# Coupling the rows of each pair once, before the substitution, in the 32x32 inverses of a delta-rule kernel

## The chip, the cores and the metric

The kernel runs on one core of a Trainium2 chip. The metric is the device time of one execution in microseconds, the median of several runs. The engines are named as in the profile: PE is TensorE (matmuls), PEld its weight loads, DVE is VectorE, ACT is ScalarE, POOL is GpSimd, SP is the engine that issues most of the transfers. Each engine works through its own list of instructions in order; the engines wait for each other by semaphores.

## The reference, cut to what matters

One layer of a decoder: 2048 prompt tokens with 1024 channels and 8 sample tokens go through one wide input projection, then through two branches, an RWKV-7 recurrence over 16 heads of 64 channels and a causal convolution with 31 taps, which are gated, added and projected. The change lies in the recurrence:

```python
def wkv7_scan(s0, r, w, k, v, a, b):
    """S_t = S_{t-1} diag(w_t) + (S_{t-1} a_t) b_t^T + v_t k_t^T ;  y_t = S_t r_t"""
    def step(s, inp):
        rt, wt, kt, vt, at, bt = inp
        sa = jnp.einsum('bhij,bhj->bhi', s, at)
        s = s * wt[:, :, None, :] + sa[..., None] * bt[:, :, None, :] + vt[..., None] * kt[:, :, None, :]
        yt = jnp.einsum('bhij,bhj->bhi', s, rt)
        return s, yt
```

The kernel takes the tokens in chunks of 64. Inside a chunk each token's `sa` depends on those of the tokens before it through a strictly lower triangular 64x64 matrix L of products of the a and b rows, so that the inverse of (I - L) is needed for every chunk and head. It is built from the inverses of its two 32x32 diagonal blocks and one product for the block below them. Row t of such an inverse is e_t plus the sum over s < t of L[t, s] times row s: a forward substitution over 32 rows.

## The kernel before

**Tiling.** The prompt is cut into 4 blocks of 512 tokens (`b`), a block into 8 units (`j`) of two heads, 128 channels; so there are 32 units, each with 8 chunks and 2 heads. For a unit, `unit_in` projects r, k, v and the gate (matmuls `pg<-ht,w`, each of three passes over a split into a rounded part and its remainder, 8 tiles deep) and shifts them by a token on ScalarE and VectorE (`raw`). `unit_a` makes decays and keys, the triangular matrices `W` (tile `sc`), the inverses (tiles `gd`, `gp`, `zr`, `zbuf`) and what depends on them only by chunk; `unit_b` runs the state from chunk to chunk (`xs<-pc`) and ends the branch. Between units, `fill` gives other work to the engines: `glu`, `conv_norm`, `conv_gate`, `gate`, and the taps of the convolution, which `pull` deals out on VectorE (`et`). After the 8 units of a block come `merge` and `stage_out`, nearly pure matmul stages. The 8 sample tokens are worked on by `decode` on VectorE in blocks 1 and 2.

**Order.** The program is written unit by unit, but each engine's list is laid down by a planner when the program is built: it takes the instruction with the best priority among those that it thinks ready, on estimates of its own of how long each takes. The priority is the place in the program; `later(n)` puts instructions n places back, `tc.high_priority(n)` n places ahead. The shifts, the GLU and the gates' first steps stand 550 places ahead (`HPS`, `HPU`, `HPG`, `HPZ`), `conv_norm` 200 places back (`LN`), `decode` 500 back (`LD`). So instructions of other helpers stand in VectorE's list between the steps of a substitution, and projection matmuls stand in TensorE's list while it lasts.

**The inverses, L581 to L611.** ScalarE copies the 32x32 diagonal blocks out of `W` into `gd` (L586). One transpose on VectorE (L589) lays them out as `gp[p, t, s]`: the 128 partitions are 4 quadrants (2 heads, 2 diagonal blocks) of 8 chunks with 4 partitions each, and all 4 partitions of a system hold its whole 32x32 matrix. The result `zr[p, i, t]` has 8 of the 32 columns in each of these partitions, column 4 i + d in partition d. L590 sets the diagonal of `gp` to 1, so that the unit vectors in `zr` (L594) come along in each sum. `sub` keeps the 16 entries that couple the second row of a pair to its first, `gp[2 m + 1, 2 m]` (L598), and L599 clears them in `gp`. Then the loop of L600 takes two rows at a time. For rows t and t + 1 one product (L603, tile `gd`, since `pr` lies in it) multiplies all earlier rows with the two rows of `gp`, one reduce (L605) sums over s, and one scalar_tensor_tensor (L606; in the profile L107, `zr<-zr,sub`) adds `sub` times row t to row t + 1. Only `n` of the 8 column groups and `w` of the 32 rows are touched, so that a step grows from 8 to 512 elements. Every step needs the one before it: 15 products, 15 reduces and 16 scalar_tensor_tensor in a row. Two more transposes, L609 and L611, put the result back, and the matmuls `pb<-gd,sc` (L619) are the first that need it.

**Around it.** `zr` has one buffer: GpSimd clears it for the next unit (L593) when L609 has read it, and ScalarE then writes the unit vectors (L594). `pr` and `gd` are one tile with one buffer, and `gp` is one tile with one buffer too.

Of the kernel before, what the change touches and what calls it, by code (L numbers as in the profile page):

```python
# [11 lines left out]
ALU = mybir.AluOpType  # L12
AX = mybir.AxisListType
# [13 lines left out]
def rwkv7_conformer_step(  # L27
# [6 lines left out]
    nc = tc.nc  # L34
# [55 lines left out]
    def new(shape, tag, dt=F32):  # L90
        return sb.tile(shape, dt, name=tag, tag=tag, bufs=BUFS.get(tag, 1))
# [8 lines left out]
    def tt(out, a, b, op):  # L100
        return nc.vector.tensor_tensor(out=out, in0=a, in1=b, op=op)  # L101

    def mul(out, a, b):
        return tt(out, a, b, ALU.mult)

    def stt(out, a, s, b, op0, op1):
        return nc.vector.scalar_tensor_tensor(out=out, in0=a, scalar=s, in1=b, op0=op0, op1=op1)  # L107

    def vcp(out, in_):
        return nc.vector.tensor_copy(out=out, in_=in_)  # L110
# [91 lines left out]
    for e in range(2):  # L202
        s = slice(e * 64, e * 64 + 64)
# [13 lines left out]
    with later(LI):  # L217
# [3 lines left out]
                                axis=AX.X, op=ALU.add)  # L221
        par_p = const.tile([128, 2], F32, name="par_p")
        nc.vector.tensor_reduce(out=par_p, in_=ident.rearrange("p (c d) -> p d c", d=2),
                                axis=AX.X, op=ALU.add)
        par_c = const.tile([128, 2], F32, name="par_c")
        nc.vector.tensor_reduce(out=par_c, in_=ident.rearrange("p (d c) -> p d c", d=2),
                                axis=AX.X, op=ALU.add)
# [275 lines left out]
    def unit_a(b, j, tw, ins):  # L503
# [63 lines left out]
        for hf in range(2):  # L567
            pse = [pa(), pa()]
            for i in range(4):
                c = hf * 4 + i  # L570
# [10 lines left out]
        pr = new([128, 8, 2, 32], "gd")  # L581
# [5 lines left out]
        gp = new([128, 32, 32], "gp")  # L587
        gpf = gp.rearrange("p a b -> p (a b)")
        nc.vector.transpose(out=gp, in_=gd.rearrange("p c j -> p j c").unsqueeze(3).to_broadcast([128, 32, NC, 4]))  # L589
        nc.vector.memset(gpf[:, 0:1024:33], 1.0)  # L590

        zf = new([128, 288], "zr")
        nc.gpsimd.memset(zf, 0.0)  # L593
        cp(zf.rearrange("p (i r) -> p i r", r=36)[:, :, 0:4], grp.unsqueeze(1).to_broadcast([128, 8, 4]))  # L594
        zr = zf[:, 0:256].rearrange("p (i t) -> p i t", t=32)

        sub = new([128, 16], "sub")
        vcp(sub, gpf[:, 32:1024:66])  # L598
        nc.vector.memset(gpf[:, 32:1024:66], 0.0)  # L599
        for t in range(0, 32, 2):  # L600
            n, w = t // 4 + 1, t + 2
            if t:
                mul(pr[:, 0:n, :, 0:w], zr[:, 0:n, 0:w].unsqueeze(2).to_broadcast([128, n, 2, w]),  # L603
                    gp[:, t:t + 2, 0:w].unsqueeze(1).to_broadcast([128, n, 2, w]))
                nc.vector.tensor_reduce(out=zr[:, 0:n, t:t + 2], in_=pr[:, 0:n, :, 0:w], axis=AX.X, op=ALU.add)  # L605
            stt(zr[:, 0:n, t + 1:t + 2], zr[:, 0:n, t:t + 1], sub[:, t // 2:t // 2 + 1], zr[:, 0:n, t + 1:t + 2],  # L606
                ALU.mult, ALU.add)
        zt = gd
        nc.vector.transpose(out=zt.rearrange("p c (i d) -> p i c d", d=4), in_=zr)  # L609
        zv = zbuf[u % 2]  # L610
# [32 lines left out]
        for hf in range(2):  # L643
            ps = pa()
            for i in range(4):
                nc.tensor.transpose(out=ps[:, i * 128:i * 128 + 128],
                                    in_=bk[:, hf * 4 + i, 0:2].rearrange("p a t -> p (a t)"), identity=ident)
# [518 lines left out]
    for b in range(NB):  # L1166
        last = b == NB - 1
        orr = []
        if b == SB - 1:
            work = sample_work()  # L1170
            act(gate_s, gate_s, AF.Exp, scale=-1.0)
            act(gate_s, gate_s, AF.Ln, bias=1.0)
            act(gate_s, gate_s, AF.Exp, scale=-1.0)
        parts = unit_a(b, 0, tw, ins)
        ins = unit_in(b, 1, ht)
        for j in range(HP):
            if j == RJ and not last:
                stage_rms(b + 1)
            orr.append(unit_b(b, j, parts))
            pull(FT)  # L1180
            if j < HP - 1:
                parts = unit_a(b, j + 1, tw, ins)
            if j < HP - 2:
                ins = unit_in(b, j + 2, ht)
            for what in (FILL0 if b == 0 else FILL2 if last else FILL1)[j]:
                fill(b, ht, cs, what)
                pull(FT)
            if b in DW:
                for _ in range(DW[b][j]):
                    with later(LD):  # L1190
                        next(work, None)
# [81 lines left out]
```

## Time and profile before

| | |
|---|---|
| median of 3 runs | 2832.91 us (2832.56 to 2835.99) |
| the profiled execution | 2830.14 us |
| its span, first to last instruction | 2828.4 us |
| mean granted clock of TensorE | 0.987 |
| moved to and from memory | 466.91 MB, 165 GB/s |

The profile is that of one execution. Its busy times are sums over the span and hide which stage is limited by what; its waits tell which engine stood still, and what ended that. A matmul's row is longer than the distance from one to the next, since matmuls overlap. A line such as L107 or L113 is that of a helper which all callers share, so that a group is known by the tiles beside it: `zr<-zr,sub` writes `zr` and reads `zr` and `sub`. In the views, `x480` is a count, and behind the second bar stands the engine's idle time in front of the group's instructions.

### The profile page before, as it was taken

What the parts mean: (1) busy time and instruction counts of PE and PEld (TensorE: products, weight loads), DVE (VectorE), ACT (ScalarE), POOL (GpSimd) and SP (SyncE); (2) the same over time, 40 slices, a digit from 0 to 9 for tenths busy, and PEclk for the clock granted to TensorE, in tenths of its full rate; (3) what the DMA queues carried; (4) which work ended last, traced back from release to release, by engine and by line L of the source; (5) the groups of instructions that cost most, each with busy time, mean ns of one, the idle gap of its engine ahead of it and who ended that gap; (6) DMA issues with size and microseconds to landing.
All of it is one profiled execution on the core that took longest, in us unless ns stands there. A gap on an engine that the chain in (4) does not pass through costs nothing.

```text
span 2828.4 us, 55917 instructions
## 1 busy us (share of the span) xinstructions
PE 2680.2 (95%) x22800; PEld 2129.1 (75%) x22800; DVE 1965.0 (69%) x4560; ACT 1318.7 (47%) x2783; POOL 16.1 (1%) x61
## 2 busy tenths in 40 slices
PE   6999898999999989999999998999999997999988
PEld 6888887878877767777887766777797765777777
DVE  5789898677877667667568667676665767765522
ACT  5555556662344464555113556555312455545511
POOL 0000000000000000000000000000000000000000
PEclk9999999999999999999999999999999998999999
DMA  5555754547964334254665335344475422332474
GB/s 197 202 172 189 209 179 137 182 160 249 316 240 136 105 122 136 100 168 160 215 239 202 106 103 151 116 138 162 160 237 205 156 88 71 108 117 98 135 275 161
DMA packets 153107, 466.91 MB, mean 165 GB/s; under 512 B 19281, under 2 KB 24642, under 8 KB 152843
## 3 DMA queue, kind: packets, MB, share of 16 engines
q1 hardware_dynamic: 145745, 437.55, 46.3%
q10 hardware_dynamic: 7106, 25.79, 2.5%
q8 instruction: 179, 2.93, 0.4%
q14 instruction: 77, 0.63, 0.1%
HBM read 350.41 MB, written 113.35 MB: 164 GB/s over the span
## 4 chain that ended last, share of the span: by engine, by line
PE 53%; DVE 29%; ACT 13%; issue 3%; DMA 2%; SPq 0%; POOL 0%; DVEq 0%; ACTq 0%; POOLq 0%
PE pg L113 34%; PE pa L113 7%; DVE gd L101 5%; DVE zr L605 5%; PE pc L113 4%; PE py L113 4%; DVE zr L107 3%; DVE et L107 3%; ACT sc L95 2%; PE pb L113 2%; DVE raw L107 2%; ACT zbuf L95 2%; ACT xv L95 1%; DVE w L101 1%; ACT tmp L95 1%
## 5 line engine op out<-in xcount | busy, mean ns | idle before, releaser
L113 PE MATMUL pg<-ht,w 128*128 128x512 f32 (+1 forms) x7200 | 1518.6, 362 | 15.1 <-DVE sraw L110 5.3
L113 PEld LDWEIGHTS pg<-ht,w 128*128 128x128 f32 x7200 | 1163.2, 189 | 255.5 <-issue 59.8
L107 DVE SCALAR_TENSOR_TENSOR et<-u,cw,et 128x512 f32<-128x512 f32 x480 | 359.4, 749 | 6.7
L95 ACT ACTIVATE raw<-pg,omm 128x512 f32<-128x512 f32 (+1 forms) x155 | 92.9, 602 | 208.9 <-PE pg L113 201.4
L95 ACT ACTIVATE tmp<-tmp 128x512 f32<-128x512 f32 (+1 forms) x305 | 185.0, 625 | 9.0 <-DVE tmp L526 3.2
L101 DVE TENSOR_TENSOR gd<-zr,gp 128x8 f32<-128x8 f32 (+14 forms) x480 | 179.7, 374 | 11.7
L113 PE MATMUL pg<-orr,w 128*128 128x512 f32 (+2 forms) x960 | 185.0, 349 | 0.0
L605 DVE TENSOR_REDUCE zr<-gd 128x2 f32<-128x8 f32 (+14 forms) x480 | 176.6, 368 | 11.7
L113 PEld LDWEIGHTS pg<-orr,w 128*128 128x128 f32 x960 | 155.2, 188 | 25.1
L95 ACT ACTIVATE w<-wraw 128x512 fp32r<-128x512 f32 x162 | 101.3, 627 | 117.8 <-PE pg L113 75.4
L698 DVE TENSOR_SCALAR xs<-pc,dk 128x64 f32<-128x64 f32 x224 | 63.5, 284 | 111.6 <-PE pc L113 109.3
L95 ACT ACTIVATE sc<-pa 64x256 f32<-64x256 f32 (+1 forms) x192 | 72.9, 380 | 136.4 <-PE pb L113 133.1
L101 DVE TENSOR_TENSOR w<-wraw,w 128x512 fp32r<-128x512 f32 x162 | 111.0, 687 | 32.2 <-ACT w L95 31.5
L107 DVE SCALAR_TENSOR_TENSOR raw<-pg,prm,raw 128x511 f32<-128x511 f32 (+1 forms) x185 | 104.3, 574 | 29.9 <-ACT raw L95 29.3
L107 DVE SCALAR_TENSOR_TENSOR zr<-zr,sub 128x5 f32<-128x5 f32 (+7 forms) x512 | 115.7, 226 | 13.3
L95 ACT ACTIVATE gd<-sc 32x128 f32<-32x128 f32 x256 | 78.4, 306 | 92.2 <-DVE sc L101 89.6
L101 DVE TENSOR_TENSOR x<-x,pg 128x512 f32<-128x512 f32 (+1 forms) x80 | 46.2, 578 | 94.6 <-PE pg L113 56.5
L113 PE MATMUL pa<-ar,bk 64*64 64x128 f32 x2048 | 105.7, 285 | 5.6 <-DVE sc L101 3.2
L113 PEld LDWEIGHTS pa<-ar,bk 64*64 64x64 f32 x2048 | 81.3, 136 | 39.2 <-DVE bk L101 15.2
L101 DVE TENSOR_TENSOR sc<-pa,maskw 128x512 f32<-128x512 f32 x128 | 82.7, 685 | 30.8 <-PE pa L113 30.7
L101 DVE TENSOR_TENSOR keep<-pa,raw 128x512 f32<-128x512 f32 x32 | 22.1, 692 | 113.9 <-PE pa L113 113.9
L113 PE MATMUL pg<-xv,w 128*128 128x512 f32 (+2 forms) x320 | 89.8, 354 | 8.8 <-DVE x L101 8.8
(360 smaller groups left out, 3654.3 us busy)
## 6 DMA issues: line engine op xcount, KB each, us to landing
w<-kept_in SPq DMA_DIRECT2D x366, 512.0 KB, 3.3
kept_in<-w SPq DMA_DIRECT2D x122, 512.0 KB, 4.0
wraw<-in_w_in_dram SPq DMA_DIRECT2D x122, 256.0 KB, 3.2
w<-kept_br SPq DMA_DIRECT2D x48, 512.0 KB, 4.1
w<-kept_out SPq DMA_DIRECT2D x40, 512.0 KB, 4.3
gate<-x ACTq DMA_DIRECT2D x32, 512.0 KB, 4.9
x<-gate SPq DMA_DIRECT2D x64, 256.0 KB, 3.9
w<-kept_bc SPq DMA_DIRECT2D x24, 512.0 KB, 3.5
```

The lines of the kernel that those rows point to most:

```text
L95: return nc.scalar.activation(out=out, in_=in_, func=func, scale=scale, bias=bias, **kw)
L101: return nc.vector.tensor_tensor(out=out, in0=a, in1=b, op=op)
L107: return nc.vector.scalar_tensor_tensor(out=out, in0=a, scalar=s, in1=b, op0=op0, op1=op1)
L113: return nc.tensor.matmul(out=out, lhsT=lhsT, rhs=rhs, start=start, stop=stop, **kw)
L605: nc.vector.tensor_reduce(out=zr[:, 0:n, t:t + 2], in_=pr[:, 0:n, :, 0:w], axis=AX.X, op=ALU.add)
L698: nc.vector.tensor_scalar(out=state[:, j, :] if c == NC - 1 else xs[:, c + 1, :], in0=pu[:, c * C:c * C + C], scalar1=dk[:, c:c + 1], scal ...
```

## The change

The coupling inside each pair is put into the rows of `gp` once, ahead of the loop. For all 16 pairs together, one product makes coupling times first row (into `pr`, 128x16x32), and one addition adds it to the second row. This is done before the diagonal is set to 1, so that the coupling entry itself stays in `gp` and brings in the unit vector of row t; it is no longer cleared. With that, a step's product and reduce give both rows of the pair at once, and the scalar_tensor_tensor is left at t = 0 alone, where there is no product. The copy `sub` and the memset that cleared the entries go.

```diff
         nc.vector.transpose(out=gp, in_=gd.rearrange("p c j -> p j c").unsqueeze(3).to_broadcast([128, 32, NC, 4]))
+
+        both = pr.rearrange("p a b c -> p (a b) c")
+        rows2 = gp.rearrange("p (r i) s -> p r i s", i=2)
+        mul(both, rows2[:, :, 0, :], gpf[:, 32:1024:66].unsqueeze(2).to_broadcast([128, 16, 32]))
+        tt(rows2[:, :, 1, :], rows2[:, :, 1, :], both, ALU.add)
         nc.vector.memset(gpf[:, 0:1024:33], 1.0)
...
-        sub = new([128, 16], "sub")
-        vcp(sub, gpf[:, 32:1024:66])
-        nc.vector.memset(gpf[:, 32:1024:66], 0.0)
-        for t in range(0, 32, 2):
+        stt(zr[:, 0:1, 1:2], zr[:, 0:1, 0:1], gpf[:, 32:33], zr[:, 0:1, 1:2], ALU.mult, ALU.add)
+        for t in range(2, 32, 2):
             n, w = t // 4 + 1, t + 2
-            if t:
-                mul(pr[:, 0:n, :, 0:w], zr[:, 0:n, 0:w].unsqueeze(2).to_broadcast([128, n, 2, w]),
-                    gp[:, t:t + 2, 0:w].unsqueeze(1).to_broadcast([128, n, 2, w]))
-                nc.vector.tensor_reduce(out=zr[:, 0:n, t:t + 2], in_=pr[:, 0:n, :, 0:w], axis=AX.X, op=ALU.add)
-            stt(zr[:, 0:n, t + 1:t + 2], zr[:, 0:n, t:t + 1], sub[:, t // 2:t // 2 + 1], zr[:, 0:n, t + 1:t + 2],
-                ALU.mult, ALU.add)
+            mul(pr[:, 0:n, :, 0:w], zr[:, 0:n, 0:w].unsqueeze(2).to_broadcast([128, n, 2, w]),
+                gp[:, t:t + 2, 0:w].unsqueeze(1).to_broadcast([128, n, 2, w]))
+            nc.vector.tensor_reduce(out=zr[:, 0:n, t:t + 2], in_=pr[:, 0:n, :, 0:w], axis=AX.X, op=ALU.add)
```

## The prediction

> **What bounds the kernel now.** I read the page first: the busy times, then the chain that ended last.
>
> ```profile
> span 2828.4 us, 55917 instructions
> ...
> PE 2680.2 (95%) x22800; PEld 2129.1 (75%) x22800; DVE 1965.0 (69%) x4560; ACT 1318.7 (47%) x2783; POOL 16.1 (1%) x61
> ...
> PE 53%; DVE 29%; ACT 13%; issue 3%; DMA 2%; SPq 0%; POOL 0%; DVEq 0%; ACTq 0%; POOLq 0%
> PE pg L113 34%; PE pa L113 7%; DVE gd L101 5%; DVE zr L605 5%; PE pc L113 4%; PE py L113 4%; DVE zr L107 3%; DVE et L107 3%; ACT sc L95 2%; PE pb L113 2%; DVE raw L107 2%; ACT zbuf L95 2%; ACT xv L95 1%; DVE w L101 1%; ACT tmp L95 1%
> ```
>
> The two views seem to disagree. By busy time TensorE is the bound: it is idle for 2828.4 − 2680.2 = 148 us in all. By the chain, the substitution (gd L101, zr L605, zr L107) holds 5 + 5 + 3 = 13% of the span, some 370 us, on VectorE. Both can be true: a chain follows whoever came last, even by a fraction of a microsecond, and says nothing of how little earlier TensorE could have gone on. So the waits of TensorE decide, and next to them the stretches in which TensorE has work at hand.
>
> ```profile
> PEld pb L113 <- DVE gd L609: 31.2, 27, 4.6
> PE pb L113 <- DVE gd L609: 20.2, 22, 4.1
> ...
> PE pg L113 <- DVE tmp L101: 26.1, 6, 7.0
> ...
> ACT zr L95 <- POOL zr L593: 50.8, 7, 13.1
> ```
>
> (Columns: total us, number of waits, longest.) The end of the substitution is the transpose L609. TensorE waited for it 20.2 us in 22 of the 32 units, 4.1 us at most; its weight loads, which run ahead of the matmuls, 31.2 us. That is what TensorE loses to the substitution in the whole program, out of a chain share of some 370 us. The timeline of TensorE during the substitution shows why; here are the last unit, one with much other VectorE work in between, and an early one:
>
> ```profile
> 2639.63 15.34 PE L113 MATMUL pg<-ht,w 128*128 128x512 f32 x65
> 2656.29 0.69 PE L113 MATMUL pb<-gd,sc 32*32 32x32 f32 x32 [1.32 <-DVE gd L609]
> ...
> 1723.70 2.08 PE L113 MATMUL pg<-tmp,avg_c 128*128 128x512 f32 x2 [6.61 <-DVE tmp L101]
> 1724.79 20.10 PE L113 MATMUL pg<-ht,w 128*128 128x512 f32 x80
> 1745.06 0.69 PE L113 MATMUL pb<-gd,sc 32*32 32x32 f32 x32 [0.16 <-DVE gd L609]
> ...
> 160.57 23.67 PE L113 MATMUL pg<-ht,w 128*128 128x264 f32 x192 [0.17 <-DVE u L107]
> 184.41 0.60 PE L113 MATMUL pg<-ht,w 128*128 128x264 f32 x3 [0.17 <-DVE sraw L110]
> 184.93 0.69 PE L113 MATMUL pb<-gd,sc 32*32 32x32 f32 x32
> ```
>
> Ahead of the first matmul that needs the inverse stands a run of projection matmuls: 65 here, 80 there, 192 narrower ones in the third. TensorE comes to the waiting matmul 1.32 us early, 0.16 us early, or not early at all. The fill is fitted to the length of each substitution: the planner that lays down each engine's order puts in as many matmuls as it thinks the VectorE work lasts. A wait of 1 us is what its estimate misses.
>
> **What the change removes and adds.** For each of 32 units it takes away 15 of the 16 scalar_tensor_tensor (the one at t = 0 stays), the copy of sub and one memset, and adds a product and an addition of 512 elements each: 17 instructions out, 2 in. The durations:
>
> ```profile
> L107 DVE SCALAR_TENSOR_TENSOR zr<-zr,sub 128x5 f32<-128x5 f32 (+7 forms) x512 | 115.7, 226 | 13.3
> ...
> L110 DVE COPY sub<-gp x32: 136/138/141, 90.9 to 2639.2; 128x16 f32<-128x16 f32 x32
> ...
> L599 DVE MEMSET gp<- x32: 72/72/72, 91.1 to 2639.4; 128x16 f32 x32
> ...
> 2637.86 1.25 DVE L589 STREAM_TRANSPOSE gp<-gd 128x1024 f32<-128x1024 f32 x1 [0.73 <-ACT gd L95]
> 2639.18 0.14 DVE L110 COPY sub<-gp 128x16 f32<-128x16 f32 x1
> 2639.20 0.09 DVE L590 MEMSET gp<- 128x32 f32 x1
> 2639.38 0.20 DVE L107 SCALAR_TENSOR_TENSOR zr<-zr,sub 128x1 f32<-128x1 f32 x1
> 2639.40 0.07 DVE L599 MEMSET gp<- 128x16 f32 x1
> 2639.61 0.17 DVE L101 TENSOR_TENSOR gd<-zr,gp 128x8 f32<-128x8 f32 x1
> 2639.81 0.16 DVE L605 TENSOR_REDUCE zr<-gd 128x2 f32<-128x8 f32 x1
> 2640.01 0.22 DVE L107 SCALAR_TENSOR_TENSOR zr<-zr,sub 128x1 f32<-128x1 f32 x1
> 2640.26 0.18 DVE L101 TENSOR_TENSOR gd<-zr,gp 128x24 f32<-128x24 f32 x1
> ...
> 2654.07 0.69 DVE L101 TENSOR_TENSOR gd<-zr,gp 128x512 f32<-128x512 f32 x1
> 2654.80 0.69 DVE L605 TENSOR_REDUCE zr<-gd 128x16 f32<-128x512 f32 x1
> 2655.52 0.23 DVE L107 SCALAR_TENSOR_TENSOR zr<-zr,sub 128x8 f32<-128x8 f32 x1
> 2655.79 0.45 DVE L609 STREAM_TRANSPOSE gd<-zr 128x256 f32<-128x256 f32 x1
> ```
>
> Busy time: 480 × 0.226 = 108.5 us go, with 32 × (0.138 + 0.072) = 6.7 us; the two new operations have no row of their own, the nearest is the 128x512 product above at 0.69 us (same operation, broadcast operands, SBUF), so 64 × 0.69 = 44.2 us come. VectorE falls by 71 us to about 1894 us.
>
> Length of one substitution, in the last unit, where nothing else runs on VectorE: from the end of L589 (2637.86 + 1.25 = 2639.11) to the end of L609 (2655.79 + 0.45 = 2656.24) it is 17.13 us. A scalar_tensor_tensor that goes frees the time to the next start: 2640.26 − 2640.01 = 0.25 in the first such step, 2655.79 − 2655.52 = 0.27 in the last; 15 × 0.26 = 3.9 us. At the head the first one now starts at 2639.38; with the new pair ahead, each holding the next by 0.73 as the product does at 2654.07 (the reduce starts at 2654.80), it starts at 2639.18 + 2 × 0.73 = 2640.64, so 1.26 later. Saved: 3.9 − 1.26 = 2.6 us, a chain of 14.5 us. A bound for the pair, whose rows are picked out with a stride that no row shows:
>
> ```profile
> L107 DVE SCALAR_TENSOR_TENSOR et<-u,cw,et 128x512 f32<-128x512 f32 x480 | 359.4, 749 | 6.7
> ```
>
> At the 0.749 us of this dearer two-step operation of the same size the saving is 0.1 us smaller; the cheapest the pair can be is nothing, and then 1.4 us more are saved. I keep 2.6. The diagonal memset, now behind the pair, costs 0.02 to 0.2 us (2639.18 to 2639.20, or to the next start at 2639.38), inside that bound. No DMA, no ScalarE and no matmul instruction is added or moved. The new product writes the tile that ScalarE filled for L589, which the same engine has read by then, so no wait across engines is added. ScalarE's wait for zr (50.8 us, through GpSimd's memset) hangs on L609 of the unit before and ends sooner with it; it is at no place that TensorE shows as a wait of its own.
>
> **What of it reaches the end.** 32 × 2.6 = 84 us would be saved if TensorE stood still meanwhile. It does not:
>
> ```profile
> core 0: us, PE busy (x) PEld busy (x) DVE busy (x) ACT busy (x) POOL busy (x), PEclk, DMA share, GB/s
> ...
> 640.00:820.00 180.00, 180.00 (x786) 146.96 (x785) 138.37 (x215) 59.65 (x113) 0.00 (x0) 1.00 0.84 292
> ...
> 2639.10:2656.25 17.15, 15.87 (x71) 12.51 (x69) 15.40 (x51) 3.39 (x5) 0.00 (x0) 1.00 0.55 184
> ```
>
> In the 17.15 us of the last substitution TensorE is busy for 15.87, and its 65 matmuls take 15.34 / 65 = 0.236 us each, against 180.0 / 786 = 0.229 us in a stage that does nothing but such matmuls. There is no slack inside that run; only its end, the 1.28 us, can be won. The Trainium skill, "Perfetto Trace Analysis", section Identifying the Most-Contended Engine, holds that matmul busy time is a bad measure of how far TensorE is from its limit and that the share of weight loads should be read. By that share (75% on the page) TensorE would have a quarter of its time free, and the whole 84 us could be had. The rows above speak against it here: the pure matmul stage has weight loads busy for only 146.96 of 180.00 us, 82%, with TensorE never idle.
>
> So the gain is bounded by the waits on L609. If every engine kept its order, each wait would shrink by up to 2.6 us: all 20.2 us except 4.1 − 2.6 = 1.5 of the longest, so 18.7 us (29 us if the weight loads' 31.2 tells the truth). If the order is planned anew, the fill shrinks with the chain, and what remains is how far the plan misses. Were the miss in proportion to the number of the chain's instructions (in a unit 15 products and 15 reduces, the groups below over 32, and 16 scalar_tensor_tensor), removing 15 of 46 would take 33% of 20.2 us, 6.7 us.
>
> ```profile
> L101 DVE TENSOR_TENSOR gd<-zr,gp 128x8 f32<-128x8 f32 (+14 forms) x480 | 179.7, 374 | 11.7
> ...
> L605 DVE TENSOR_REDUCE zr<-gd 128x2 f32<-128x8 f32 (+14 forms) x480 | 176.6, 368 | 11.7
> ```
>  The last unit, with nothing between, misses by 1.32 us, the unit of 20.10 us of fill by 0.16: it is the short steps, not the length, that are underrated, it seems, which puts the value above 6.7. I take the middle of 6.7 and 18.7, 13 us. The matmuls that leave the fill cost nothing; they stand later, where others stand now.
>
> The profiled execution took 2830.14 us, its span and 1.7 us around it; with 13 us less, 2817. It lies 2.8 us below the median of the runs, 2832.91, so for the median 2820.
>
> **The rivals.** (1) The order does not move: 18.7 us, 2814. For it: the priorities are the same and only 15 instructions of a unit go. Against: the fills above follow each chain's length.
> (2) The plan swallows it: the estimates follow the chain, the wait stays about 20 us, the median stays at 2833, within 5.7 us. For it: the wait is much the same in chains of very different fill. This is also how it goes if the new pair, at the head, is dearer than I think.
> (3) The whole chain comes through: 84 us, 2749. For it only the chain of waits; against it the 15.87 busy us.
> (4) Slower: the wait on the convolution's sums. conv_norm's additions share VectorE with one substitution in each block:
>
> ```profile
> 1045.67 0.68 DVE L101 TENSOR_TENSOR tmp<-tmp 128x512 f32<-128x512 f32 x1
> 1046.27 0.22 DVE L107 SCALAR_TENSOR_TENSOR zr<-zr,sub 128x3 f32<-128x3 f32 x1
> ```
>
> TensorE waits for these sums 26.1 us in 6 places, 6.61 us in the row at 1723.70, where its mean-matmul stands ahead of 80 projection matmuls that could run. The new pair is two long operations at the head of just that stretch, and the priorities reach 550 places in a program that is now 15 places shorter per unit, so the plan there can turn. If these waits double, 26 us are lost against 13 won: 2846. It decides once they grow by more than 13; from 19 on the kernel is measurably slower.
>
> **How the numbers follow.** A measurement of this kernel tells 0.2%, 5.7 us. Chances: the forecast 0.38 (its own range 2814 to 2826, from 18.7 to 6.7 us), the fixed order 0.18, the swallowed gain 0.27, the whole chain 0.04, slower 0.13. Faster by over 0.2%: 0.38 + 0.18 + 0.04 = 0.60; the same 0.27; slower 0.13. The range takes in the fixed order with the weight loads' 29 us (2804) and the swallowed gain with its 5.7 us (2839); it leaves out the chain and nearly all of the slower case.
>
> **What would show it.** Two new rows x32 at about 0.69 us, the scalar_tensor_tensor down to x32, a substitution with nothing between of 14.5 us, VectorE at about 1894 us: these test the cost. TensorE's busy time unchanged at 2680 and the wait on the transpose at 7 us instead of 20.2 test the forecast; a wait near 1.5 with the same 65 matmuls ahead of it would be rival 1, a wait near 20 with some 11 matmuls fewer (2.6 / 0.236) rival 2, a longer row of waits for tmp rival 4. The forecast is wrong if the time moves while the wait on the transpose does not.

## The result and the profile after

The kernel after takes 2804.84 us in the median of 4 runs (2802.72 to 2806.61), beside 2834.45 us for the kernel before on the same chip (2832.56 to 2838.42): a ratio of 0.989, with an interval of 0.9878 to 0.9902. That is 29.6 us less, where 13 were forecast; the time lies just inside the low end of the range, 2804 to 2839. The two profiled executions, 2830.14 and 2806.61 us, are 23.5 us apart, since the first is shorter than each of the four timed runs of its kernel and the second is the longest of its own. What follows from the traces accounts for those 23.5 us; the other 6 are in no trace here.

The page of the kernel after, span, busy times and chain:

```profile
span 2804.9 us, 55406 instructions
...
PE 2681.7 (96%) x22800; PEld 2131.4 (76%) x22800; DVE 1906.5 (68%) x4080; ACT 1321.7 (47%) x2783; POOL 16.4 (1%) x61
...
PE 61%; DVE 22%; ACT 12%; DMA 2%; issue 2%; SPq 0%; POOL 0%; DVEq 0%; ACTq 0%; POOLq 0%
PE pg L113 43%; PE pa L113 7%; DVE gd L101 5%; PE pc L113 4%; PE py L113 4%; DVE zr L606 4%; PE pb L113 2%; ACT sc L95 2%; DVE et L107 2%; ACT zbuf L95 1%; DVE raw L107 1%; ACT gd L95 1%; ACT keep L95 1%; ACT xv L95 1%; DVE gp L589 1%
```

TensorE has the same matmuls and the same busy time (2680.2 before, 2681.7 now), so the whole gain is time in which TensorE stood still. VectorE's share of the chain fell from 29% to 22%; the entry `zr L107`, 3% before, is gone.

The substitution itself, from the timeline of VectorE in the last unit (start, duration, instruction):

```profile
2608.14 1.25 DVE L589 STREAM_TRANSPOSE gp<-gd 128x1024 f32<-128x1024 f32 x1 [0.73 <-ACT gd L95]
2609.42 0.69 DVE L101 TENSOR_TENSOR gd<-gp 128x512 f32<-128x512 f32 x1
2610.15 0.69 DVE L101 TENSOR_TENSOR gp<-gp,gd 128x512 f32<-128x512 f32 x1
2610.92 0.19 DVE L107 SCALAR_TENSOR_TENSOR zr<-zr,gp 128x1 f32<-128x1 f32 x1
2610.94 0.09 DVE L595 MEMSET gp<- 128x32 f32 x1
2611.14 0.17 DVE L101 TENSOR_TENSOR gd<-zr,gp 128x8 f32<-128x8 f32 x1
2611.34 0.16 DVE L606 TENSOR_REDUCE zr<-gd 128x2 f32<-128x8 f32 x1
2611.54 0.18 DVE L101 TENSOR_TENSOR gd<-zr,gp 128x24 f32<-128x24 f32 x1
...
2623.35 0.45 DVE L608 STREAM_TRANSPOSE gd<-zr 128x256 f32<-128x256 f32 x1
```

From the end of L589 (2609.39) to the end of L608, the old L609 (2623.80), it is 14.4 us, where 17.13 stood. Between a reduce and the next product there is no instruction any more. TensorE in the same stretch:

```profile
2609.93 13.26 PE L113 MATMUL pg<-ht,w 128*128 128x512 f32 x56
2623.85 0.69 PE L113 MATMUL pb<-gd,sc 32*32 32x32 f32 x32 [0.67 <-DVE gd L608]
```

The fill has shrunk with the chain, from 65 matmuls to 56, and the wait at its end from 1.32 to 0.67 us. So far the prediction holds. Its waits do not; here are those of TensorE:

```profile
PE pa L414 <- DVE orr L107: 15.1, 1, 15.1
PE pb L113 <- DVE gd L608: 14.0, 15, 5.0
PE pg L113 <- DVE x L101: 10.0, 1, 10.0
PE pg L113 <- DVE tmp L101: 9.3, 4, 6.9
```

The wait on the transpose fell by 6.2 us only (20.2 to 14.0), and the wait on the convolution's sums by 16.8 (26.1 to 9.3), though the change does not touch these sums; part of the latter came back under other names.

Where the time went shows in the view of stretches: those of blocks 1, 2 and 3 from the end of one output stage to the start of the next merge, 24 of the 32 units. TensorE has the same 4725, 4645 and 4485 instructions between these bounds in each kernel (a count in a row can hold one or two more that straddle an edge). Before, and then after:

```profile
801.80:1358.90 557.10, 535.82 (x4727) 401.57 (x4726) 402.64 (x981) 283.43 (x601) 2.70 (x8) 0.99 0.43 141
1491.20:2035.10 543.90, 520.46 (x4647) 388.46 (x4646) 380.32 (x930) 280.15 (x596) 2.70 (x8) 0.99 0.44 142
2180.80:2696.50 515.70, 484.65 (x4487) 362.57 (x4485) 338.88 (x812) 259.09 (x541) 2.36 (x7) 0.98 0.35 119
sum 1616.70, PE 1540.93 PEld 1152.60 DVE 1121.84 ACT 822.67 POOL 7.76; mean PE 513.64 PEld 384.20 DVE 373.95 ACT 274.22 POOL 2.59
```

```profile
798.80:1350.80 552.00, 539.40 (x4727) 404.89 (x4726) 381.14 (x855) 284.02 (x601) 2.70 (x8) 0.98 0.44 142
1483.00:2023.00 540.00, 521.83 (x4646) 390.20 (x4645) 364.23 (x810) 281.23 (x596) 2.70 (x8) 0.99 0.43 143
2168.80:2673.10 504.30, 482.94 (x4486) 358.49 (x4484) 320.88 (x691) 259.53 (x541) 2.36 (x7) 0.99 0.36 122
sum 1596.30, PE 1544.17 PEld 1153.59 DVE 1066.24 ACT 824.78 POOL 7.76; mean PE 514.72 PEld 384.53 DVE 355.41 ACT 274.93 POOL 2.59
```

The first figure behind the window is its length, the next TensorE's busy time. The stretches are 20.4 us shorter, of the 23.5 in all. TensorE's idle time in them is 1616.70 − 1540.93 = 75.8 us before and 1596.30 − 1544.17 = 52.1 after: 23.6 less, of which 3.2 return as longer busy time. This idle figure is what the experiments below are read by. Split by what ended each wait, the 75.8 us before were 18.6 on the transpose, 17.3 on the convolution's sums (`tmp`), and some 40 in small waits on a dozen other tiles; after, they are 8.1, 8.9 and 35, of which 7.3 are on `bk`, a tile of the keys. The labels are not separate accounts: a stall can keep its place and change its name, as is shown further down.

### The profile page after: what moved, and what is told of

Read it like the earlier page. It is cut to its first block, busy times and chain, and to the rows that moved or that the text cites. A ratio compares the mean times of both kernels' runs of the same rounds, so it can differ in the third digit from the quotient of the medians.

```text
span 2804.9 us, 55406 instructions
## 1 busy us (share of the span) xinstructions
PE 2681.7 (96%) x22800; PEld 2131.4 (76%) x22800; DVE 1906.5 (68%) x4080; ACT 1321.7 (47%) x2783; POOL 16.4 (1%) x61
## 4 chain that ended last, share of the span: by engine, by line
PE 61%; DVE 22%; ACT 12%; DMA 2%; issue 2%; SPq 0%; POOL 0%; DVEq 0%; ACTq 0%; POOLq 0%
PE pg L113 43%; PE pa L113 7%; DVE gd L101 5%; PE pc L113 4%; PE py L113 4%; DVE zr L606 4%; PE pb L113 2%; ACT sc L95 2%; DVE et L107 2%; ACT zbuf L95 1%; DVE raw L107 1%; ACT gd L95 1%; ACT keep L95 1%; ACT xv L95 1%; DVE gp L589 1%
## 5 line engine op out<-in xcount | busy, mean ns | idle before, releaser
L107 DVE SCALAR_TENSOR_TENSOR et<-u,cw,et 128x512 f32<-128x512 f32 x480 | 359.0, 748 | 7.6
L107 DVE SCALAR_TENSOR_TENSOR raw<-pg,prm,raw 128x511 f32<-128x511 f32 (+1 forms) x185 | 103.6, 573 | 44.1 <-ACT raw L95 43.1
L95 ACT ACTIVATE x<-pg 128x512 f32<-128x512 f32 (+1 forms) x80 | 40.7, 509 | 137.6 <-PE pg L113 136.9
```

The lines of the kernel that those rows point to most:

```text
L95: return nc.scalar.activation(out=out, in_=in_, func=func, scale=scale, bias=bias, **kw)
```

## The experiments

The first theory was that the shorter chain brings the gain by more than the wait on the transpose shows (A). Its rival: the planner laid the program out anew, and the new order happened to suit the convolution's sums (B). Later two forms of A stood against each other: the gain goes by the chain's length (C), or by the number of short steps, which the planner underrates (D). Last came VectorE's load: it fell too, so that anything that waits for VectorE might come sooner. Each run's ratio is to the kernel before on the same chip.

**Other orders of the kernel before.** e1 moves the work that runs ahead by 15 places, as many instructions as the change takes from a unit; e2 halves the distance by which the convolution's norm is put back.

```diff
-HP = 550
+HP = 565
```

> The substitution of before, with the 550 places of priority made 565, so that the same work is put in another order (about a seventh of TensorE's list changes). Theory A, the shorter VectorE chain itself makes the gain: nothing of the work has changed, so the time stays at 2834 us within 5 us. Theory B, over half of the gain is the new order that came with the change (the waits on the convolution's sums fell from 26.1 to 9.3 us without being touched): a new order alone moves the time, by 8 us or more either way.

Measured: 2830.53 us, ratio 0.9976 (0.9963 to 0.9989).

```diff
-LN = 200
+LN = 100
```

> The substitution of before, with the convolution's normalisation put 100 places back instead of 200: again the same work in another order. Theory A: 2834 us within 5 us. Theory B: it moves by 8 us or more, together with the wait of TensorE on the convolution's sums.

Measured: 2832.82 us, ratio 0.9992 (0.9983 to 1.0002). In both, TensorE's idle time in the three stretches stayed where it was, 75.2 and 76.1 us, and the wait on the sums moved little, 26.8 and 22.5 us.

**The sums put first**, in the kernel before (e3) and the kernel after (e4):

```diff
+HN = 1000
...
+        with tc.high_priority(HN):
+            for ct in range(CT):
+                tt(cs[ct], cs[ct], ps, ALU.subtract)
...
+            ps = stat(pgt, avg_c, sm)
```

> The substitution of before, with the squares and sums of the convolution's normalisation put 1000 places ahead, so that they no longer stand between the steps of a substitution in VectorE's list. Theory B: TensorE's wait on these sums (24 us in four blocks) shrinks to a few us and the kernel gains about 17 us, 2817 us, with the long substitution still in it. Theory A: these waits are no part of the gain, at most 5 us are won, 2830 us or more.

> The changed kernel with the same sums put ahead. What is left there is a wait of 6.9 us on the sums in one block and 5.0 us in another, where the sum's matmul stands right ahead of the inverse's. Theory B: both go, 2793 us. Theory A: no change, 2805 us within 4 us.

Measured: e3 2839.88 us, ratio 1.0013 (1.0002 to 1.0025); e4 2812.05 us, ratio 0.992 (0.9905 to 0.9935). The waits on the sums, e3 and then e4 (the program is one line longer):

```profile
PE pg L114 <- DVE tmp L102: 20.1, 6, 7.1
PE pb L114 <- DVE gd L610: 19.8, 20, 4.1
```

```profile
PE pb L114 <- DVE gd L609: 8.4, 15, 0.9
PE pg L114 <- DVE tmp L102: 8.4, 3, 7.0
```

In e3 the wait on the sums fell from 26.1 to 20.1 us only, little more than in e2, and in e4 one stall of 5.86 us at a sums' matmul in block 2 is put down to a DMA instead, so the pair says little of what the sums' wait is worth. But e3 is a third order of the same work, and it gains nothing either.

**A new order of the kernel after** (e11), with the norm 185 places back instead of 200:

```diff
-LN = 200
+LN = 185
```

> The changed kernel's work in another order (the convolution's normalisation 185 places back instead of 200, which undoes the 15 instructions by which a unit is shorter; a tenth of TensorE's list moves). C and D: 2805 us within 8 us, as the runs of before's work in other orders stayed within 0.3%. If the order that came with the change is what gained: slower than the changed kernel by 10 us or more.

Measured: 2807.32 us, ratio 0.9897 (0.9884 to 0.991). Three orders of the long chain lie between 0.9976 and 1.0013, three of the short one (after, e4, e11) between 0.989 and 0.992. So B is not borne out: no order tried brought the old kernel near the new one, and the gain survived in all orders of the new one. The order alone moves either by up to 0.3%.

**Half of the coupling** (e5): the pair of operations treats only the last 8 pairs, and the first 8 keep their scalar_tensor_tensor. The chain of a unit is 15.63 us.

```diff
-        mul(both, rows2[:, :, 0, :], gpf[:, 32:1024:66].unsqueeze(2).to_broadcast([128, 16, 32]))
+        mul(both[:, 8:16], rows2[:, 8:16, 0, :], gpf[:, 32 + 8 * 66:1024:66].unsqueeze(2).to_broadcast([128, 8, 32]))
...
+            if t < 16:
+                stt(zr[:, 0:n, t + 1:t + 2], zr[:, 0:n, t:t + 1], sub[:, t // 2:t // 2 + 1],
+                    zr[:, 0:n, t + 1:t + 2], ALU.mult, ALU.add)
```

> Only the last 8 of the 16 pairs are coupled beforehand (two operations on 256 elements); the first 8 keep their scalar_tensor_tensor. The chain of one substitution: 8 x 0.26 us less, 2 x 0.46 us more at the head, about 1.2 us shorter than before's 17.1, or 16.0 us; 8 of the 46 short steps go. Theory C, the time follows the length of the chain (2.7 us per unit gave 30 us, so about 11 us of time per us of chain): 13 us faster than before, ratio 0.995. Theory D, it follows the number of short steps, whose duration the planner underrates (15 of them gave 30 us): 16 us faster, ratio 0.994. Chance of the order: anything within 8 us of before.

Measured: 2828.43 us, ratio 0.9973 (0.9961 to 0.9985), half of what either theory wanted. Idle time in the stretches fell to 62.9 us, but a single wait of 9.1 us on the transpose came up:

```profile
PE pb L113 <- DVE gd L614: 20.4, 16, 9.1
...
PE pg L113 <- DVE tmp L101: 12.0, 5, 7.2
```

**The pair and the short steps** (e6): the two new operations, and 15 scalar_tensor_tensor with a zero scalar left in their places. The chain is 18.37 us.

```diff
             nc.vector.tensor_reduce(out=zr[:, 0:n, t:t + 2], in_=pr[:, 0:n, :, 0:w], axis=AX.X, op=ALU.add)
+            stt(zr[:, 0:n, t + 1:t + 2], zr[:, 0:n, t:t + 1], zero[:, 0:1], zr[:, 0:n, t + 1:t + 2], ALU.mult, ALU.add)
```

> The pair of the change at the head, but the 15 scalar_tensor_tensor stay in the chain, with a scalar of zero, so that the result is the same: the chain is 1.3 us longer than before's (18.4 us), the number of short steps is that of before. Theory C: 1.3 x 11 = 14 us slower than before, ratio 1.005. Theory D: as before within 5 us, ratio 1.000, with the wait on the transpose back at 1.3 us in the last unit.

Measured: 2838.34 us, ratio 1.0011 (0.9998 to 1.0024). Its profiled execution, 2847.98 us, is the longest of its ten, so its rows are not leaned on. The 1.24 us that the pair adds to a unit's chain cost 3 us in all, and the interval takes in no change. That is what D expected; C in its strict form wanted 14 us.

**The steps as a load beside the chain** (e7): 15 scalar_tensor_tensor in each unit, on constants, needed by nobody, 300 places back.

```diff
+            with later(300):
+                stt(dead[:, 0:n], zero[:, 0:n], zero[:, 0:1], zero[:, 0:n], ALU.mult, ALU.add)
```

> The changed kernel, and on VectorE beside it the 15 scalar_tensor_tensor of each unit as dead work on constants that nothing waits for, 300 places later in priority: VectorE's busy time is 108 us above the changed kernel's while no step of the chain needs them. If the gain is one of VectorE's load, it goes: 2832 us, ratio 0.999. If it is one of the chain (C or D), most of it stays: 2805 to 2812 us, ratio 0.990.

Measured: 2827.38 us, ratio 0.9971 (0.996 to 0.9981). This did not test what it was made for. Work on constants is ready from the start, and the planner pulled it there: block 0 with the start took 686.5 us instead of 666.9, with this wait ahead of it where 15.1 us stood, while the three stretches stayed as in the kernel after (1599.3 us, idle 55.2):

```profile
PE pa L417 <- DVE orr L107: 24.0, 1, 24.0
```

**A far shorter chain** (e8): the loop begins at row 18, so that rows 2 to 17 of each inverse are left out, and the chain is 10.07 us.

```diff
-        for t in range(2, 32, 2):
+        for t in range(18, 32, 2):
```

> The changed kernel with the loop begun at row 18, so that 8 products and 8 reduces of each substitution are left out (the inverse is then not computed in its upper rows): the chain loses the 16 cheapest steps, about 5 us, to 9.5 us. Theory C: 5 x 11 = 55 us faster than the changed kernel, 2750 us, ratio 0.970. Theory D: the 16 of 31 short steps take half of what is left of the waits on the transpose and the sums (14.0 and 9.3 us), 10 to 15 us, 2792 us, ratio 0.985.

Measured: 2786.86 us, ratio 0.9828 (0.9813 to 0.9842). Idle time in the stretches fell to 42.6 us, and the waits on transpose and sums all but went:

```profile
PE pg L113 <- DVE tmp L101: 4.2, 2, 3.9
PE pb L113 <- DVE gd L608: 4.0, 12, 0.5
```

Eight passes of the loop fewer bring 49 us, some 18 more than the change, for 4.33 us less chain a unit: the gain per microsecond of chain has fallen. C in its strict form had wanted 55 us more than the change, D 10 to 15.

**Few steps, the same length** (e9): the coupling is put into groups of four rows, so that 16 products and reduces are left instead of 30, paid for by four more operations of 512 elements at the head. The chain is 14.95 us, half a microsecond longer than after's.

```diff
+        for j in range(2):
+            mul(four, quad[:, :, j:j + 1, :].to_broadcast([128, 8, 2, 32]),
+                diag[:, :, 64 + j:97 + j:32].unsqueeze(3).to_broadcast([128, 8, 2, 32]))
+            tt(quad[:, :, 2:4, :], quad[:, :, 2:4, :], four, ALU.add)
...
-        for t in range(2, 32, 2):
+        for t in range(0, 32, 4):
```

> The changed kernel carried one step on: after the pairs, rows 2 and 3 of each four get the coupling to rows 0 and 1 by two products and two additions of 512 elements, and the loop takes four rows at a time. 30 short steps become 16 (the sum of their elements is the same), four long operations come at the head; by the rows of the changed kernel the chain stays about as long, 14.4 to 15 us. Theory C (length): no gain over the changed kernel, ratio to before 0.989 to 0.991. Theory D (number of short steps that the planner underrates): 14 steps fewer at 0.6 to 1.5 us of TensorE's waits each over the program give 8 to 20 us, ratio 0.982 to 0.986, and the wait on the transpose in the last unit falls from 0.67 us to about 0.4 us.

Measured: 2815.85 us, ratio 0.9931 (0.9917 to 0.9945); the stretches are those of after (1598.6 us, idle 55.0). With 16 steps instead of 30 there is no more gain than the length allows, so D fails here.

**Load behind the chain** (e10): 15 scalar_tensor_tensor in each unit again, but reading the finished inverse, so that they cannot move to the start.

```diff
+        with later(100):
+            for _ in range(15):
+                stt(dead, zv[:, :, 32], zero[:, 0:1], zero, ALU.mult, ALU.add)
```

> The changed kernel with 15 scalar_tensor_tensor of dead work per unit that read the finished inverse, so that they can't run early as in the run before, and 100 places later in priority: VectorE's load of before, spread over the program, with the chain left short. If the load makes the time, the gain is lost in good part: 2825 us or more, ratio 0.996. If the steps inside the chain make it (C, D): 2804 to 2812 us, ratio 0.989 to 0.992.

Measured: 2816.65 us, ratio 0.9929 (0.9913 to 0.9945). VectorE is busier here than in the kernel before:

```profile
PE 2683.7 (95%) x22800; PEld 2140.2 (76%) x22800; DVE 2002.1 (71%) x4560; ACT 1321.2 (47%) x2783; POOL 16.2 (1%) x63
```

Yet two thirds of the gain are there, by the ratios 20 of 31 us. So load is not what the gain came from, although 96 us more of it, behind the chain, cost some 11 us (the wait on the sums is 21.6 us).

**Less load, the same chain** (e14): the kernel before with six taps of the convolution left out.

```diff
-        for tap in range(1, NTAP):
+        for tap in range(7, NTAP):
```

> Before, with 6 of the convolution's 30 multiply-add taps left out on VectorE (16 x 6 x 0.749 = 72 us less load; the convolution is then computed with fewer taps), the chain unchanged. Load theory: as fast as the changed kernel, 2805 us, ratio 0.990. Chain theory: 8 us or less are won, 2826 us, ratio 0.997, with the wait on the transpose at about 20 us.

Measured: 2836.98 us, ratio 1.0005 (0.9995 to 1.0015).

```profile
PE 2688.0 (95%) x22800; PEld 2135.4 (75%) x22800; DVE 1907.8 (67%) x4464; ACT 1320.1 (47%) x2783; POOL 16.1 (1%) x61
```

VectorE is as busy as in the kernel after (1906.5 us), and nothing is gained; idle time in the stretches is 74.6 us.

**The chain unhooked.** In e12, made from the kernel before, and e13, from the kernel after, the substitution runs in full, and so do the matmuls and copies behind it, but these read a constant tile and write scratch tiles. Nobody waits for the inverse any more.

```diff
-                mm(ps[hi[e], c * 32:c * 32 + 32], W[c // 4][lo[e], c % 4, e, 32:64], zt[lo[e], c, :])
+                mm(ps[hi[e], c * 32:c * 32 + 32], W[c // 4][lo[e], c % 4, e, 32:64], zfix[lo[e], c, 0:32])
...
-            cp(zv[lo[e], :, 32:64], ps[lo[e], 0:NC * 32].rearrange("p (c t) -> p c t", t=32))
+            cp(zscr[lo[e]], ps[lo[e], 0:NC * 32].rearrange("p (c t) -> p c t", t=32))
...
-        return W, ar, aw, xv, zv, dk, bonv, sz
+        return W, ar, aw, xv, zfix, dk, bonv, sz
```

> Before's substitution runs on VectorE in full, but the matmuls and copies behind it read a constant tile in place of the inverse (the recurrence is then computed with a wrong inverse): VectorE's load is before's, the chain no longer holds anything. If the chain is what costs, this gains at least the wait on the transpose and more, 2790 us or less, ratio 0.984 or lower. If VectorE's load is what costs, little changes: 2825 us or more, ratio 0.997.

> The same with the changed kernel's substitution. Against the run before it differs by VectorE's load alone, 58 us less by the traces of the two kernels. Chain theory: the two unhooked kernels lie within 8 us of each other, since the load counts little (dead work of 96 us cost about 11 us, so 58 us would be some 7 us). Load theory: this one is faster by 20 us or more.

Measured: e12 2775.06 us, ratio 0.9781 (0.9765 to 0.9797); e13 2772.96 us, ratio 0.9776 (0.9762 to 0.9791). The sums over the three stretches, e12 and then e13:

```profile
sum 1572.70, PE 1550.91 PEld 1163.47 DVE 1099.42 ACT 827.08 POOL 7.79; mean PE 516.97 PEld 387.82 DVE 366.47 ACT 275.69 POOL 2.60
```

```profile
sum 1569.90, PE 1550.52 PEld 1163.65 DVE 1056.01 ACT 827.67 POOL 7.79; mean PE 516.84 PEld 387.88 DVE 352.00 ACT 275.89 POOL 2.60
```

Two things follow. With nothing hanging on the substitution the old and the new one take the same time, although VectorE's load differs by 57 us (1949.8 and 1892.9 over the span): this difference in load counts for nothing by itself. And the dependence on the inverse costs the kernel before 2.2%, 62 us. This price takes in the matmuls and copies that hand the inverse on, since their result is waited for no more either; it is an upper bound of what a shorter substitution can bring. Of the 62 us the traces show 47, since the profiled execution of before is a short one and that of e12, 2783.14 us, the longest of its four. In the stretches unhooking takes 54.0 of the 75.8 us of idle time away (1572.70 − 1550.91 = 21.8 are left), of which the rows labelled with the transpose held 18.6. The 17.3 us on the convolution's sums go to 0.4 with them, although not one instruction of these sums was touched; 10 of the 54 us come back as longer busy time of the same matmuls.

**All lengths side by side**, each change as the ratio times its own median of before (by the medians alone after is −30). The length is that of the last unit, where nothing else runs on VectorE:

| chain of a unit | kernel | change of the time |
|---|---|---|
| 18.37 us | e6 | +3 us |
| 17.13 us | before | 0 |
| 17.13 us, other orders | e1, e2, e3 | −7, −2, +4 us |
| 17.13 us, less load | e14 | +1 us |
| 15.63 us | e5 | −8 us |
| 14.95 us | e9 | −20 us |
| 14.40 us | after | −31 us |
| 14.40 us, other orders | e4, e11 | −23, −29 us |
| 14.40 us, more load | e7, e10 | −8, −20 us |
| 10.07 us | e8 | −49 us |
| not waited for | e12, e13 | −62, −64 us |

Leaving the kernels with other load aside, the time falls with the length, so A stands, although neighbouring rows lie within the scatter that other orders make. C in its strict form, a fixed gain per microsecond, does not stand: after gains 31 us for 32 × 2.73 = 87 us of chain, a third; e5 a sixth of its 48; e8 a fifth of its 226. That scatter, up to 8 us, is as large as most of these departures. In most units other work of VectorE stands between the steps, and there the chain fell by more: from the end of L589 to the end of the transpose that ends the substitution the mean of the 32 units is 23.1 us before and 19.0 after. The curve also has a floor: some 62 us are all there is to win at this place.

## Why the prediction was right about the cost and wrong about what reaches the end

**The cost of the parts: right.** Pair at 0.69 us each, here as groups of the whole program:

```profile
L101 DVE TENSOR_TENSOR gd<-gp x32: 679/691/693, 92.9 to 2609.4; 128x512 f32<-128x512 f32 x32
L101 DVE TENSOR_TENSOR gp<-gp,gd x32: 681/691/693, 93.6 to 2610.2; 128x512 f32<-128x512 f32 x32
```

The chain came out at 14.4 us (14.5 forecast), the saving at 2.73 instead of 2.6 us a unit.

**VectorE's busy time: 1906.5 instead of 1894 us.** The rows of all its instructions add up to 76.9 us less, a little more than the 71 forecast. But they overlap, and busy time counts an overlap once: the rows sum to 2160.7 us where the page says 1965.0. What went was in part overlapped, like the copy and the memset at 2639.18 and 2639.20. Taking durations off a busy time overstated what went. It changed nothing in the forecast, which gave this load no price; e12 and e13 bear that out.

**The fill follows the chain: right.** 56 matmuls where 65 stood, and the wait at their end half as long. That the matmuls that leave it cost nothing is right too: TensorE's busy time is the same.

**"So the gain is bounded by the waits on L609": the step that failed.** From it came the 13 us, and both ends of the forecast's own range. The gain, 29.6 us, is larger than all the 20.2 us that TensorE's waits held under this name, and of these only 6.2 went (the weight loads' 31.2 us fell by 6.4). The view of waits names for each wait the one that came last. It does not say what would have been there sooner, had the chain been shorter. e12 measured that: the dependence on the inverse cost 62 us. The rest was booked under the convolution's sums, `aw`, `zbuf`, `xv`, and others.

The sums can be followed in the timeline of TensorE. These are their two pairs of matmuls in block 2, in the kernel before and then in e12:

```profile
1716.07 1.02 PE L113 MATMUL pg<-tmp,avg_c 128*128 128x512 f32 x2
1723.70 2.08 PE L113 MATMUL pg<-tmp,avg_c 128*128 128x512 f32 x2 [6.61 <-DVE tmp L101]
```

```profile
1711.64 1.12 PE L113 MATMUL pg<-tmp,avg_c 128*128 128x512 f32 x2
...
1713.60 2.15 PE L113 MATMUL pa<-sc,pz 64*64 64x128 f32 x32
1715.68 1.15 PE L113 MATMUL pc<-xv,sc 128*64 128x64 f32 x30
...
1722.75 1.12 PE L113 MATMUL pg<-tmp,avg_c 128*128 128x512 f32 x2 [0.15 <-DVE tmp L101]
```

In the kernel before, nothing stands between the two pairs. The additions of the sums stand in VectorE's list between the steps of the substitution; the unit's next matmuls need the inverse and start at 1745.06 only; and the 80 projection matmuls that TensorE has until then stand behind the second pair. In e12 matmuls of the unit that no longer wait for the inverse (`pa<-sc,pz`, `pc<-xv,sc` and more) fill this place. The sums come no sooner there, 11.1 us behind the first pair instead of 7.6, and yet nobody waits for them. So the wait bears the name of the sums, but it lasts, at least in part, because the inverse holds back what could stand in it. Why the planner put the 80 matmuls behind the second pair is not shown. The copies to `zbuf` and the matmuls behind them are the next steps after the transpose, and the waits on these (5.6 us in the stretches before, 4.5 after) cannot arise in e12, where 1.1 us stand for the scratch tile in their place.

The expected fall of the wait on the transpose, to 7 us, was wrong in the same way, and the middle value of 13 us rested on short steps being underrated, which e9 did not bear out. The wait is 14.0, of which 5.0 is a single place in block 0, in the timeline of TensorE of the kernel after:

```profile
465.06 1.02 PE L113 MATMUL pg<-tmp,avg_c 128*128 128x512 f32 x2
471.04 1.06 PE L113 MATMUL pb<-gd,sc 32*32 32x32 f32 x32 [4.96 <-DVE gd L608]
```

No projection matmul stands between the two. In the kernel before, the second pair of the sums' matmuls stands at this place and waits 7.00 us. Block 3 shows the same change of name, before and then after:

```profile
2390.59 2.08 PE L113 MATMUL pg<-tmp,avg_c 128*128 128x512 f32 x2 [5.74 <-DVE tmp L101]
```

```profile
2364.27 1.13 PE L113 MATMUL pg<-tmp,avg_c 128*128 128x512 f32 x2 [1.12 <-DVE tmp L101]
2371.30 0.69 PE L113 MATMUL pa<-ar,bk 64*64 64x128 f32 x4 [5.90 <-DVE bk L101]
```

So of the 16.8 us by which the sums' wait fell, some 11 came back right beside it, 5.0 under the transpose and 5.9 under `bk`. Waits of this kind, 5 to 9 us each, come and go with the order; that they make much of the scatter between versions is likely, but not shown.

**Luck.** That the time lies inside the wider range is luck. Its low end, 2804, took the 29 us of the weight loads' waits for an order that does not move; the order moved, and these waits fell by 6.4.

**The rivals.** The fixed order (18.7 us) fell by the fill's 56; its bound was the same rows and had the same fault. The swallowed gain fell. The whole chain, 84 us, fell as the rows of the pure matmul stage said: a third of it came. The rule of the Trainium skill ("Perfetto Trace Analysis", section Identifying the Most-Contended Engine), by which the share of weight loads tells how far TensorE is from its limit, would have led there. The traces go on speaking against it: the share hardly moved (75% to 76%), and in e12, with no one waiting for the inverse, TensorE is busy for 97% of the span with weight loads at 77%:

```profile
PE 2697.3 (97%) x22800; PEld 2148.1 (77%) x22800; DVE 1949.8 (70%) x4560; ACT 1324.8 (48%) x2783; POOL 16.2 (1%) x62
```

The slower case did not come: the sums' wait did not double, it fell, though in good part by a change of name.

**What stays open.** How the 23.6 us less of idle time in the stretches divide by cause, since the labels change places; why the gain of e5 is so small and after's so near to half of all there is; and the 6 us between the pair of profiled executions and the medians. e4, the kernel after with the sums put first, gains 23 us, so some 8 of the 31 may be this order's own.

## What to carry to other kernels

The label on a wait tells who came last, not what a chain costs: the rows of one line are no upper bound for what shortening its chain can bring. To price a chain, unhook it: let its work run in full, but give its readers a constant, and read what the program then takes; that is an upper bound for what shortening it can bring. Before believing or doubting a gain of a per cent in a kernel whose order is planned, time a few other orders of the same work; here they spread by 0.3%.

## What the runs showed of the hardware that was not expected

The two operations that pick every second row of a 32x32 matrix, one of them with a broadcast operand picked out at a stride of 66, took 0.691 us in the median, against 0.684 for the plain additions of the same size (`tmp<-tmp` 128x512 f32): the stride cost next to nothing. And the same matmuls at nearly the same mean granted clock (0.987 before, 0.988 in e12) were busy for 2680.2 us with gaps between them and 2697.3 us without: part of a closed gap came back as busy time here, 10 of 54 us in the three stretches.
